# Splitting the forms of a pair of weight blocks as three tiles of 1024 columns and one of 512

## The chip, the core and the metric

The kernel runs on one core of a Trainium2 chip, in one launch. The metric is the device time of one execution in microseconds, here the median of several runs. TensorE (PE in the profile, its weight loads PEld) does the matmuls, VectorE is DVE, ScalarE is ACT, GpSimd is POOL, and SyncE (SP) issues most DMAs.

## The reference

The kernel computes one layer of a hybrid encoder on 512 positions of width 1024, in float32:

```python
x1 = x  + RMSNorm( W_out( sig(a_ret) * W_ret_o(Retention(h)) + sig(a_sgu) * W_sgu_o(SGU(h)) ) ),  h = RMSNorm(x)
y  = x1 + RMSNorm( ConvGatedMLP( RMSNorm(x1) ) )
```

`h @ w_in` gives the queries, keys, values and gate of the retention branch, the two inputs `u` and `sv` of the SGU branch, and the two merge gates. The SGU branch is `(gelu(u) * mixed(sv)) @ w_sgu_o`, the gated MLP is `gelu(a) * b` of an up projection (2 x 2816 columns, with a convolution of width 3), followed by `w_down`. Nearly all of the time is matrix products of 512 positions with weights.

## The kernel before

**High and low parts.** A float32 product is made of three matmuls of float32r operands. `split(hi, lo, src)` (line 119 and the copy of line 100) rounds a tile on ScalarE, `hi = copy(src)`, and takes the rest on VectorE, `lo = src - hi`. Each weight tile in use is a pair (hi, lo), and each product does hi by hi, hi by lo and lo by hi.

**Weights in a ring.** The weights come as 146 blocks of 128 x 1024 float32, each by one DMA of 512 KB into one of four `raw` tiles, issued on SyncE. Their halves go into a ring of nine slots of 1088 columns (tag `w4`). `w_get` hands out the units of a list in the order of their use, and starts on the units ahead as far as the ring has room: nine slots in general. A whole block takes two slots (one for hi, one for lo).

**Pairs.** Where two weight blocks that stand side by side make two tiles of outputs, the class `Pair` uses a scheme with 7 products in place of 8, in the manner of Strassen and Winograd. Its weights are seven forms of 128 x 512: B11, B21, the sums T1 = B11 + B12, T3 = B12 + B22, T2 = T1 + B22, T4 = T2 + B21, and B22. Each form is used in one product of 12 matmuls of 128 x 256 (line 926), in the order B11, B21, T1, T2 (`part1`), T3 (`part2`), T4, B22 (`part3`). There are 20 pairs, 1680 matmuls in all:

- The middle stage, some 200 to 343 us, has four pairs for `u` (U1, U2, U3 in the table `MIDDLE` are their parts 1, 2 and 3) and four for the gate (G1, G2, G3), interleaved with whole blocks (W) and small steps (M, Y). U11 and U12 are part 1 of the second and third pair for `u`.
- The gate stage, some 343 to 403 us, has four `gated_pair`: part 1, a whole block (`f_block`, lines 300 to 302), part 2, half a block, part 3, the other half.
- The up projection, some 490 to 648 us, has eight pairs in the same manner (`COUPLES`, each a pair and two whole blocks).

Then comes the down projection (line 1372), whose weights `w_down` splits (dh, dl); the change doesn't touch its code.

**How a form is made before.** `w_form` takes one ring slot for each of the seven forms, with lo and hi side by side in it, and splits 512 columns at a time. B11 brings the two DMAs of the pair. T1 and T3 are added on VectorE when T1 is due; T2 then too, on VectorE in the pairs for `u` and in the couples, on GpSimd in the gate pairs of both stages. T4 is added when it is due, on the same engine, in the place of T2.

**What sets the order.** The program is written in the order of use, and a scheduler of the compiler sets the order of each engine's instructions by its own estimate of when they may start. On one engine they then go in that order, and an instruction that has to wait for another engine (a copy on ScalarE, a slot that TensorE still reads) holds up those behind it. Part 1's products accumulate in PSUM banks; the fourth product (T2, called S2 after its second operand) is added to the bank of the first, so it must wait for ScalarE's copy of the first out of PSUM.

Of the kernel before, what the change touches and what calls it, by code (L numbers as in the profile page):

```python
# [13 lines left out]
ALU = mybir.AluOpType  # L14

P = 128
D = 1024
S = 512
# [34 lines left out]
def tile_block(ctx: ExitStack, tc, xT, x, wall, par, cs, wsp, bsp, gpost, gffn, out):  # L53
# [71 lines left out]
    FORMS = ("B11", "B21", "T1", "T2", "T3", "T4", "B22")  # L125
    units = []
    i = 0
    while i < NW:
# [6 lines left out]
        elif i == U0:  # L135
            us, gs = ([[(f, k + n * m) for f in FORMS] for n in range(KD // 2)] for k, m in ((U0, 2), (GATE0, 4)))
            ws = [("blk", GATE0 + 4 * (n // 2) + 2 + n % 2) for n in range(KD)]
            for what, n in MIDDLE:
                units += {"W": lambda: ws[n : n + 1], "U1": lambda: us[n][:4], "U2": lambda: us[n][4:],
                          "G1": lambda: gs[n][:4], "G2": lambda: gs[n][4:]}.get(what, list)()  # L140
            i = GATE0 + 2 * KD
        elif GATE0 <= i < GATE1:
            units += pair[:4] + [("blk", i + 2)] + pair[4:] + [("blk", i + 3)]
            i += 4
        elif i == UP0 + 2 * COUPLES[0][0]:
            for a, b in COUPLES:
                pair = [(f, UP0 + 2 * a) for f in FORMS]
                units += pair[:4] + [("blk", UP0 + 2 * b)] + pair[4:] + [("blk", UP0 + 2 * b + 1)]
# [45 lines left out]
    def w_form(form, i):  # L194

        if form == "B11":
            a, b = raw_tile(), raw_tile()
            nc.sync.dma_start(a, wall[i])
            nc.sync.dma_start(b, wall[i + 1])
            w_raw["B11"], w_raw["B12"] = a[:, :S], a[:, S:]  # L200
            w_raw["B22"], w_raw["B21"] = b[:, :S], b[:, S:]
        elif form == "T1":
            t = raw_tile()
            w_raw["T1"], w_raw["T2"], w_raw["T3"], w_raw["T4"] = t[:, :S], t[:, S:], w_raw["B12"], t[:, S:]
            nc.vector.tensor_add(w_raw["T1"], w_raw["B11"], w_raw["B12"])
            nc.vector.tensor_add(w_raw["T3"], w_raw["B12"], w_raw["B22"])
            eng = nc.vector if i < GATE0 or i >= UP0 else nc.gpsimd
            eng.tensor_tensor(out=w_raw["T2"], in0=w_raw["T1"], in1=w_raw["B22"], op=ALU.add)
        elif form == "T4":
            eng = nc.vector if i < GATE0 or i >= UP0 else nc.gpsimd  # L210
            eng.tensor_tensor(out=w_raw["T4"], in0=w_raw["T2"], in1=w_raw["B21"], op=ALU.add)
        w = slot("wf", 0, 1088)
        lo, hi = w[:, AT_64 : AT_64 + S], w[:, S + AT_192 : 2 * S + AT_192]
        split(hi, lo, w_raw[form])
# [66 lines left out]
    def w_size(u):  # L281
        return 2 if u[0] in ("blk", "q", "t") or u[0][0] == "s" else 1
# [626 lines left out]
    class Pair:  # L909
# [9 lines left out]
        def product(self, b, act, first, w=None):  # L919
            wh, wl = w or w_get()  # L920
# [21 lines left out]
        def part1(self):  # L942
# [3 lines left out]
            def second():  # L946
# [732 lines left out]
```

## Time and profile before

| what | value |
|---|---|
| median of 3 runs | 783.18 us (782.7 to 783.85) |
| the profiled execution, span | 782.6 us, 13472 instructions |
| TensorE clock granted, mean | 0.997 of full speed |
| TensorE busy | 774.5 us, 99% of the span |
| VectorE, ScalarE, GpSimd busy | 639.5, 485.2, 103.5 us |

In the profile a group of instructions is named by its line, engine and operation, with output and inputs by their names in the program: `wf` is a form's slot, `wh` and `wl` the halves of a whole block, `raw` a weight tile as it came, `u`, `sig` and `c` a pair's output tiles, `ps` a PSUM bank. A row such as `x140 | 107.0, 774` means 140 of them, busy for 107.0 us together, 774 ns the mean of one; what follows is idle time ahead of them and who ended it. In a timeline, a row has the start, the length in us, the engine, the line and the operation; "x2" is two that follow one another directly. Lengths of neighbours overlap, so the step from one start to the next is what an operation takes up.

### The profile page before, as it was taken

What the parts mean: (1) busy time and instruction counts of PE and PEld (TensorE: products, weight loads), DVE (VectorE), ACT (ScalarE), POOL (GpSimd) and SP (SyncE); (2) the same over time, 40 slices, a digit from 0 to 9 for tenths busy, and PEclk for the clock granted to TensorE, in tenths of its full rate; (3) what the DMA queues carried; (4) which work ended last, traced back from release to release, by engine and by line L of the source; (5) the groups of instructions that cost most, each with busy time, mean ns of one, the idle gap of its engine ahead of it and who ended that gap; (6) DMA issues with size and microseconds to landing.
All of it is one profiled execution on the core that took longest, in us unless ns stands there. A gap on an engine that the chain in (4) does not pass through costs nothing.

```text
span 782.6 us, 13472 instructions
## 1 busy us (share of the span) xinstructions
PE 774.5 (99%) x5139; PEld 720.7 (92%) x5139; DVE 639.5 (82%) x1093; ACT 485.2 (62%) x878; POOL 103.5 (13%) x132
## 2 busy tenths in 40 slices
PE   9999999999999999999999999999999999999996
PEld 8888998998999999999998998999999998999996
DVE  6567987789789988877765679989999889886987
ACT  7555568688466766644454686657777568644542
POOL 0040001130021102033211200001111012200001
PEclk9999999999999999999999999999999999999998
DMA  8783224453223233233459120435555375733344
GB/s 288 271 246 102 81 82 162 108 122 108 81 91 126 82 122 121 83 110 106 138 171 337 54 81 28 124 107 141 142 148 149 108 199 111 171 114 107 109 162 162
DMA packets 35889, 104.80 MB, mean 134 GB/s; under 512 B 4400, under 2 KB 6320, under 8 KB 35824
## 3 DMA queue, kind: packets, MB, share of 16 engines
q1 hardware_dynamic: 27936, 87.81, 34.0%
q0 software_dynamic: 7024, 14.95, 9.0%
q10 hardware_dynamic: 864, 1.18, 0.4%
q8 instruction: 40, 0.66, 0.4%
q14 instruction: 25, 0.20, 0.1%
HBM read 91.34 MB, written 4.19 MB: 122 GB/s over the span
## 4 chain that ended last, share of the span: by engine, by line
PE 92%; DVE 3%; DMA 3%; issue 1%; ACT 0%; POOLq 0%; DVEq 0%; POOL 0%; ACTq 0%
PE ps L926 24%; PE ps L300 12%; PE ps L302 12%; PE ps L301 12%; PE ps L1372 7%; PE ps L755 5%; PE ps L634 4%; PE ps L636 4%; PE ps L635 4%; DMA raw<-wall 3%; PE ps L1109 2%; PE ps L1108 2%; PE ps L1107 2%; DVE dl L119 1%; PE ps L997 1%
## 5 line engine op out<-in xcount | busy, mean ns | idle before, releaser
L119 DVE TENSOR_TENSOR wl<-raw,wh 128x1024 fp32r<-128x1024 f32 (+1 forms) x84 | 96.0, 1152 | 54.3 <-issue 19.1
L100 ACT ACTIVATE wf<-raw 128x512 fp32r<-128x512 f32 x140 | 85.6, 625 | 67.3 <-PE ps L301 19.4
L926 PE MATMUL ps<-sh,wf 128*128 128x256 f32 x640 | 117.4, 276 | 0.1
L119 DVE TENSOR_TENSOR wf<-raw,wf 128x512 fp32r<-128x512 f32 x140 | 107.0, 774 | 9.2 <-ACT wf L100 8.6
L926 PEld LDWEIGHTS ps<-sh,wf 128*128 128x128 f32 x640 | 101.9, 192 | 1.1 <-ACT sig L100 0.5
L100 ACT ACTIVATE wh<-raw 128x1024 fp32r<-128x1024 f32 (+2 forms) x88 | 84.8, 977 | 28.5 <-DMA raw<-wall 14.0
L300 PE MATMUL ps<-h2h,wh 128*128 128x512 f32 (+1 forms) x256 | 90.6, 354 | 0.0
L301 PE MATMUL ps<-h2l,wh 128*128 128x512 f32 (+1 forms) x256 | 90.4, 353 | 0.0
L302 PE MATMUL ps<-h2h,wl 128*128 128x512 f32 (+1 forms) x256 | 90.4, 353 | 0.0
L926 PE MATMUL ps<-sl,wf 128*128 128x256 f32 x320 | 88.0, 275 | 0.0
L926 PEld LDWEIGHTS ps<-sl,wf 128*128 128x128 f32 x320 | 61.4, 192 | 0.4
L1372 PE MATMUL ps<-dh,fh 128*128 128x256 f32 x216 | 59.6, 276 | 0.3 <-DVE yy L1409 0.3
L1372 PE MATMUL ps<-dl,fh 128*128 128x256 f32 x216 | 59.5, 275 | 0.0
L1372 PE MATMUL ps<-dh,fl 128*128 128x256 f32 x216 | 59.4, 275 | 0.0
L100 ACT ACTIVATE dh<-raw 128x768 fp32r<-128x768 f32 (+1 forms) x36 | 33.6, 950 | 33.8 <-DVE raw L231 15.2
L302 PEld LDWEIGHTS ps<-h2h,wl 128*128 128x128 f32 x256 | 48.6, 190 | 5.1
L301 PEld LDWEIGHTS ps<-h2l,wh 128*128 128x128 f32 x256 | 48.6, 190 | 4.5
L300 PEld LDWEIGHTS ps<-h2h,wh 128*128 128x128 f32 x256 | 48.6, 190 | 4.5
L926 PE MATMUL ps<-xh,wf 128*128 128x256 f32 x288 | 52.2, 275 | 0.0
L636 PE MATMUL ps<-wh,xl 128*128 128x512 f32 x128 | 48.5, 379 | 0.0
L635 PE MATMUL ps<-wl,xh 128*128 128x512 f32 x128 | 48.5, 379 | 0.0
L634 PE MATMUL ps<-wh,xh 128*128 128x512 f32 x128 | 48.5, 380 | 0.0
(343 smaller groups left out, 2171.6 us busy)
## 6 DMA issues: line engine op xcount, KB each, us to landing
raw<-wall SPq DMA_DIRECT2D x144, 512.0 KB, 3.7
x<-x SPq DMA_DIRECT2D x24, 256.0 KB, 6.0
fl<-gp POOLq DMA_DIRECT2D x12, 256.0 KB, 3.8
swap<-qkraw POOLq DMA_DIRECT2D x16, 128.0 KB, 4.8
x<-x POOLq DMA_DIRECT2D x8, 256.0 KB, 2.3
fl<-fs POOLq DMA_DIRECT2D x8, 256.0 KB, 4.3
xT<-xT SPq DMA_DIRECT2D x7, 256.0 KB, 5.0
xT<-xT POOLq DMA_DIRECT2D x4, 256.0 KB, 4.1
```

Of the source, the lines that this page charges most:

```text
L100: return nc.scalar.activation(out=o, in_=i, func=AF.Copy)
L119: low[0] = nc.vector.tensor_sub(lo, src, as32(hi)).ins
L300: nc.tensor.matmul(o, ah, bh, start=start, stop=False, skip_group_check=skip)
L301: nc.tensor.matmul(o, ah, bl, start=False, stop=False, skip_group_check=skip)
L302: pe_last[0] = nc.tensor.matmul(o, al, bh, start=False, stop=stop, skip_group_check=skip).ins
L634: nc.tensor.matmul(acc[t], xh[k][:, c], turns(wh[:, f]), start=k == 0, stop=False)
L635: nc.tensor.matmul(acc[t], xh[k][:, c], turns(wl[:, f]), start=False, stop=False)
L636: part_end[0] = nc.tensor.matmul(acc[t], xl[k][:, c], turns(wh[:, f]), start=False, stop=k == KD - 1)
L755: nc.tensor.matmul(bank[t], a_[:, c], turns(w_[:, f]), start=first and k == i == 0, stop=last and k == 3 and i == 2, skip_group_check=True,)
L926: self.last = nc.tensor.matmul(o, w_[:, c], a_, start=first and k == n == 0, stop=k == 3 and n == 2, skip_group_check=True,)
L1107: nc.tensor.matmul(o, ah, turns(bh), start=k == 0, stop=False)
L1372: nc.tensor.matmul(o, a_[:, c], turns(w_[:, f]), start=j == t == i == 0, stop=j == DP - 1 and i == 2 and n not in (M2, M3, M4), skip_group ...
```

## The change

The seven forms become four units: `B1` (B11 and B21 side by side, 1024 columns), `T12` (T1 and T2), `T34` (T3 and T4) and `B22`. The host puts B21 behind B11 and B12 behind B22, so that B1 is the first DMA's tile as it came. A unit of 1024 columns takes two slots, hi and lo, like a whole block, and is split by one copy and one subtraction. B22 stays as it was. A pair still takes seven slots in all, with the same DMAs and the same adds on the same engines. T3 and T4 are now written into the raw tile of B1, once that has been split, and T2 is no longer overwritten.

A whole unit is now split at once. So the first product needs B21's half split with B11's, T1's product needs T2 added, and T3's needs T4 added; a unit's two slots come free when its second product has read them. T4's half is used in part 3 only, so T34's two slots are held from part 2 to part 3, across the parts of the other pair that stand between them in the middle stage.

```diff
-    FORMS = ("B11", "B21", "T1", "T2", "T3", "T4", "B22")
+    FORMS = ("B1", "T12", "T34", "B22")
...
-                          "G1": lambda: gs[n][:4], "G2": lambda: gs[n][4:]}.get(what, list)()
+                          "G1": lambda: gs[n][:2], "G2": lambda: gs[n][2:]}.get(what, list)()
...
-        if form == "B11":
-            a, b = raw_tile(), raw_tile()
+        eng = nc.vector if i < GATE0 or i >= UP0 else nc.gpsimd
+        if form == "B1":
+            a, b = w_raw["a"], w_raw["b"] = raw_tile(), raw_tile()
             nc.sync.dma_start(a, wall[i])
             nc.sync.dma_start(b, wall[i + 1])
-            w_raw["B11"], w_raw["B12"] = a[:, :S], a[:, S:]
-            w_raw["B22"], w_raw["B21"] = b[:, :S], b[:, S:]
-        elif form == "T1":
-            t = raw_tile()
-            w_raw["T1"], w_raw["T2"], w_raw["T3"], w_raw["T4"] = t[:, :S], t[:, S:], w_raw["B12"], t[:, S:]
-            nc.vector.tensor_add(w_raw["T1"], w_raw["B11"], w_raw["B12"])
-            nc.vector.tensor_add(w_raw["T3"], w_raw["B12"], w_raw["B22"])
-            eng = nc.vector if i < GATE0 or i >= UP0 else nc.gpsimd
-            eng.tensor_tensor(out=w_raw["T2"], in0=w_raw["T1"], in1=w_raw["B22"], op=ALU.add)
-        elif form == "T4":
-            eng = nc.vector if i < GATE0 or i >= UP0 else nc.gpsimd
-            eng.tensor_tensor(out=w_raw["T4"], in0=w_raw["T2"], in1=w_raw["B21"], op=ALU.add)
-        w = slot("wf", 0, 1088)
-        lo, hi = w[:, AT_64 : AT_64 + S], w[:, S + AT_192 : 2 * S + AT_192]
-        split(hi, lo, w_raw[form])
+            w_raw["B22"], w_raw["B12"] = b[:, :S], b[:, S:]
+            raw = a
+        elif form == "T12":
+            raw = w_raw["t"] = raw_tile()
+            nc.vector.tensor_add(raw[:, :S], w_raw["a"][:, :S], w_raw["B12"])
+            eng.tensor_tensor(out=raw[:, S:], in0=raw[:, :S], in1=w_raw["B22"], op=ALU.add)
+        elif form == "T34":
+            raw = w_raw["a"]
+            nc.vector.tensor_add(raw[:, :S], w_raw["B12"], w_raw["B22"])
+            eng.tensor_tensor(out=raw[:, S:], in0=w_raw["t"][:, S:], in1=raw[:, S:], op=ALU.add)
+        if form == "B22":
+            w = slot("wf", 0, 1088)
+            lo, hi = w[:, AT_64 : AT_64 + S], w[:, S + AT_192 : 2 * S + AT_192]
+            raw = w_raw["B22"]
+        else:
+            hi, lo = slot("wf", AT_192), slot("wf", AT_64)
+        split(hi, lo, raw)
         return hi, lo
...
-        return 2 if u[0] in ("blk", "q", "t") or u[0][0] == "s" else 1
+        return 1 if u[0] == "B22" else 2
...
+        def halves(self):
+            hi, lo = w_get()
+            return [(hi[:, f], lo[:, f]) for f in (slice(0, S), slice(S, 2 * S))]
...
-            o = self.product(0, self.x(0, T0), True)
+            w = self.halves()
+            o = self.product(0, self.x(0, T0), True, w[0])
             copy(two(c0[:, T0]), o)
-            second()
-            self.product(2, self.s("S1"), True)
-            o = self.product(0, self.s("S2"), False)
+            second(w[1])
+            w = self.halves()
+            self.product(2, self.s("S1"), True, w[0])
+            o = self.product(0, self.s("S2"), False, w[1])
...
-            o = self.product(0, self.s("S3"), False)
+            w = self.halves()
+            o = self.product(0, self.s("S3"), False, w[0])
...
-            self.w = w_get(), w_get()
+            self.w = w[1], w_get()
```

Line numbers move a little: the product's matmul is line 933 after the change, the adds into a pair's outputs of lines 948, 957, 963, 972, 976 and 978 are 955, 966, 973, 982, 986 and 988.

The scheduler's order moves with it. The first place is VectorE in the middle stage, around 250 to 257 us, where the weights of U12 are made while the pairs before it end. The names' numbers differ between the two programs. Before, `wf_2755` and `wf_2763` are B11 and B21 of U12, `wf_2783` and `wf_2799` its T1 and T2:

```order
L963 TENSOR_TENSOR u_2566<-ps_2569,u_2566 128x256
L119 TENSOR_TENSOR wf_2748<-raw_2587,wf_2748 128x512
L119 TENSOR_TENSOR wf_2755<-raw_2751,wf_2755 128x512
L205 TENSOR_TENSOR raw_2779<-raw_2751 128x512
L948 TENSOR_TENSOR sig_2758<-ps_2761,sig_2758 128x256
L119 TENSOR_TENSOR wf_2763<-raw_2752,wf_2763 128x512
L206 TENSOR_TENSOR raw_2751<-raw_2751,raw_2752 128x512
L208 TENSOR_TENSOR raw_2779<-raw_2779,raw_2752 128x512
L119 TENSOR_TENSOR wf_2783<-raw_2779,wf_2783 128x512
L957 TENSOR_TENSOR sig_2758<-sig_2758,rbc_567 128x256
L119 TENSOR_TENSOR wf_2799<-raw_2779,wf_2799 128x512
```

After, `wf_2737` is the low half of B1 and `wf_2770` that of T12:

```order
L973 TENSOR_TENSOR u_2548<-ps_2551,u_2548 128x256
L1023 TENSOR_TENSOR u_2296<-mix_2701,u_2296 128x512
L205 TENSOR_TENSOR raw_2766<-raw_2732,raw_2733 128x512
L119 TENSOR_TENSOR yl_2800<-u_2295,yh_2799 128x512
L955 TENSOR_TENSOR sig_2727<-ps_2730,sig_2727 128x256
L206 TENSOR_TENSOR raw_2766<-raw_2766,raw_2733 128x512
L119 TENSOR_TENSOR wf_2710<-raw_2582,wf_2710 128x512
L966 TENSOR_TENSOR sig_2727<-sig_2727,rbc_567 128x256
L119 TENSOR_TENSOR yl_2804<-u_2296,yh_2803 128x512
L119 TENSOR_TENSOR wf_2737<-raw_2732,wf_2736 128x1024
L1001 SCALAR_TENSOR_TENSOR add_2997<-rws_1911,part,bst_2208 128x128
L119 TENSOR_TENSOR wf_2770<-raw_2766,wf_2769 128x1024
```

B11's split was the third operation from the u row on and B21's the sixth; now both are one operation, the tenth, behind T1, T2 and two splits for the next stage (`yl`).

The second place is ScalarE at the end of the middle stage, around 325 to 329 us. The last row of the first listing, and the second of the other, copies the first product of a gated pair out of PSUM (`sig<-ps`); the sigmoids belong to the pair before it. Before:

```order
L100 ACTIVATE wf_3670<-raw_3457 128x512
L1061 ACT_TABLE_LOAD
L1061 ACTIVATE sig_3435<-sig_3435 128x512
L100 ACTIVATE yh_3661<-u_3249 128x512
L1061 ACTIVATE sig_3436<-sig_3436 128x512
L100 ACTIVATE sig_3665<-ps_3667 128x256
```

After:

```order
L100 ACTIVATE wf_3616<-raw_3422 128x512
L100 ACTIVATE sig_3611<-ps_3613 128x256
L1071 ACT_TABLE_LOAD
L1071 ACTIVATE sig_3387<-sig_3387 128x512
L1071 ACTIVATE sig_3388<-sig_3388 128x512
L100 ACTIVATE yh_3607<-u_3207 128x512
```

The copy now stands ahead of the table load and the two sigmoids.

The third place is TensorE itself, just there: its matmuls are in the same order throughout, except that in this one place the product S2, which waits for that copy, has moved. Before, the three matmuls of the first step of a whole block come ahead of it:

```order
L926 MATMUL ps_3669<-sh_1687,wf_3495 128x256
L300 MATMUL ps_3748<-yh_2828,wh_3581 128x512
L301 MATMUL ps_3748<-yl_2829,wh_3581 128x512
L302 MATMUL ps_3748<-yh_2828,wl_3582 128x512
L926 MATMUL ps_3667<-sh_603,wf_3539 128x256
```

After, S2 (`ps_3613`) follows directly on the product before it:

```order
L933 MATMUL ps_3615<-sh_1687,wf_3485 128x256
L933 MATMUL ps_3615<-sl_1688,wf_3485 128x256
L933 MATMUL ps_3615<-sh_1687,wf_3486 128x256
L933 MATMUL ps_3613<-sh_603,wf_3485 128x256
L933 MATMUL ps_3613<-sl_604,wf_3485 128x256
```

S2 moved forward by three matmuls, and the block's first step behind its twelve. SyncE's and GpSimd's orders are the same before and after.

21 lines of the change are left out of this document (9 added, 12 removed).

## The prediction, as it was recorded before the changed kernel had run

> **What bounds the kernel now.** I read the page's busy times first, then TensorE's own waits, then the windows of 20 us, and last the rows at the few places where TensorE loses time.
>
> ```profile
> PE 774.5 (99%) x5139; PEld 720.7 (92%) x5139; DVE 639.5 (82%) x1093; ACT 485.2 (62%) x878; POOL 103.5 (13%) x132
> PE 92%; DVE 3%; DMA 3%; issue 1%; ACT 0%; POOLq 0%; DVEq 0%; POOL 0%; ACTq 0%
> ```
>
> TensorE is busy for 774.5 of 782.6 us and has 92% of the chain of waits. A busy TensorE may still be slow, so I look at its pace. The chain of waits has the Pair products, line 926, in long runs without a break:
>
> ```profile
> 210.36 5.36 PE ps L926 x48
> ```
>
> 5.36 / 48 is 111.7 ns from one matmul to the next, and the rows further down step by 0.11 or 0.12 as well: the matmuls go at their own pace and no weight comes late. The change leaves 5139 matmuls of the same shapes, so it can only win what TensorE loses beyond that pace. The waits of TensorE's weight loads that touch line 926 are two:
>
> ```profile
> PEld ps L926 <- ACT sig L100: 0.5, 1, 0.5
> PEld ps L926 <- ACT u L100: 0.2, 1, 0.2
> ```
>
> The windows (PE busy, PEld busy, DVE busy, ACT busy and POOL busy, then the granted clock, the DMA share and GB/s) show where a late weight would hurt first:
>
> ```profile
> 240.00:260.00 20.00, 20.00 (x161) 19.41 (x160) 19.75 (x33) 15.36 (x26) 2.48 (x2) 1.00 0.19 63
> 340.00:360.00 20.00, 20.00 (x137) 18.71 (x136) 15.59 (x22) 9.43 (x16) 5.89 (x4) 1.00 0.31 106
> 480.00:500.00 20.00, 20.00 (x117) 18.19 (x116) 20.00 (x32) 12.65 (x22) 0.00 (x0) 1.00 0.29 95
> ```
>
> VectorE is full in 240 to 260 and in 480 to 500 us, yet TensorE loses nothing there: the weights are split some us ahead of their use, and VectorE's load is work done early. So the change matters by when the halves are ready, not by how busy VectorE is.
>
> **The change part by part.** Matmuls, DMA issues, bytes and adds stay as they are. Three times in each of the 20 pairs, two splits of 512 columns become one of 1024: 60 operations fewer on VectorE and 60 fewer on ScalarE.
>
> ```profile
> L119 DVE TENSOR_TENSOR wf<-raw,wf 128x512 fp32r<-128x512 f32 x140 | 107.0, 774 | 9.2 <-ACT wf L100 8.6
> L119 DVE TENSOR_TENSOR wl<-raw,wh 128x1024 fp32r<-128x1024 f32 x72 | 88.5, 1229 | 52.6 <-issue 19.1 <-ACT wh L100 14.6 <-PE ps L926 6.3
> ```
>
> By these means a merge saves 2 x 774 - 1229 = 319 ns on VectorE: 60 of them are 19 us of busy time. The means count overlapped ends twice. By starts of neighbours, two splits take 1.20 (250.50 to 251.70 in the next rows) and one of 1024 takes 1.13 (257.85 to 258.98): 0.07 saved, 4 us in all. I take nearer 4, as the starts hold no overlap. On the time this counts 0, and ScalarE's part too, at 62% busy: TensorE's matmuls lie over both, and if they did not, VectorE's would be worth at most 19 us.
>
> The price of the change is when a half comes. B11's product used to need a split of 512 columns; now it needs one of 1024, into two ring slots instead of one, and T3 and T4 hold two slots until part 3 has used T4. By the slots' addresses and the matmuls' times, every form in the gate stage and the couples finds its slot free over 8 us ahead of need. The exceptions are U11 and U12, whose B1 is split while another pair still holds its slots. U12 comes when VectorE is full. VectorE's rows of before there (start, length, line):
>
> ```profile
> 250.16 0.41 DVE L963 TENSOR_TENSOR u<-ps,u 128x256 f32<-128x256 f32 x1
> 250.50 1.28 DVE L119 TENSOR_TENSOR wf<-raw,wf 128x512 fp32r<-128x512 f32 x2
> 251.70 0.68 DVE L205 TENSOR_TENSOR raw<-raw 128x512 f32<-128x512 f32 x1
> 252.30 0.42 DVE L948 TENSOR_TENSOR sig<-ps,sig 128x256 f32<-128x256 f32 x1
> 252.63 0.68 DVE L119 TENSOR_TENSOR wf<-raw,wf 128x512 fp32r<-128x512 f32 x1
> ...
> 257.85 1.22 DVE L119 TENSOR_TENSOR wl<-raw,wh 128x1024 fp32r<-128x1024 f32 x1
> 258.98 0.68 DVE L978 TENSOR_TENSOR u<-u,rbc 128x512 f32<-128x512 f32 x1
> ```
>
> TensorE's rows: the last read of the slot that B1's low half goes into, the first read of that half (the third matmul of U12), the first read of T12's low half, and the loss at 261.
>
> ```profile
> 252.94 0.28 PE L926 MATMUL ps<-sl,wf 128*128 128x256 f32 x1
> ...
> 257.40 0.39 PE L926 MATMUL ps<-xh,wf 128*128 128x256 f32 x2
> ...
> 260.08 0.39 PE L926 MATMUL ps<-sh,wf 128*128 128x256 f32 x2
> ...
> 261.09 0.63 PE L926 MATMUL ps<-sh,wf 128*128 128x256 f32 x2
> 261.55 0.28 PE L926 MATMUL ps<-sl,wf 128*128 128x256 f32 x1
> ```
>
> Before, B11's low half is the second split of the row at 250.50, ready at 251.78, 5.6 us ahead of 257.40. After, the program order puts eight operations between the u row of 250.16 and B1's split. An operation of 512 costs 0.60 from start to start (251.70 to 252.30), one of 256 0.33. So: 250.16 + 0.33 + 3 x 0.60 = 252.30, where the sig operation (now line 955) also starts in before; then 0.33 + 0.60 + 0.60 + 0.33 + 0.60 gives 254.76; the split ends 1.22 later, at 255.98. The slot is free after 252.94. B1 is 1.4 us early. T12's split follows after a short add (0.26) at 256.15 and ends at 257.4, 2.7 us ahead of 260.08. ScalarE's copies come earlier: it has only 15.36 of 20 us in this window. At U11 the slot's last read and the half's first read are these:
>
> ```profile
> 227.21 0.28 PE L926 MATMUL ps<-sl,wf 128*128 128x256 f32 x1
> ...
> 231.68 0.39 PE L926 MATMUL ps<-xh,wf 128*128 128x256 f32 x2
> ```
>
> The slot is free 4.4 us ahead; the same walk there puts the split's end near 229.1, an estimate, and leaves 2.6 us. **So the cost here is 0, between 0 and what a slip beyond 1.4 us would bring.**
>
> The 0.24 lost at 261 is a wait for ScalarE's copy of u out of PSUM, itself behind a gelu:
>
> ```profile
> 259.70 0.63 ACT L1052 ACTIVATE u<-u 128x512 f32<-128x512 f32 x1
> ...
> 260.92 0.37 ACT L100 ACTIVATE u<-ps 128x256 f32<-128x256 f32 x1
> ```
>
> The gelu waits for VectorE's u at 258.98. In the new order that u has three operations between it and T12's split (257.3 + 0.33 + 0.33 + 0.60 = 258.6), and the copy stands ahead of the weight copy, so it may end at 260.2 and the loss goes; if VectorE slips by 1 us, it stays. Between -0.24 and +0.3; I take -0.1.
>
> The larger loss is at 328, where TensorE waits for a copy that ScalarE makes behind a table load and two sigmoids:
>
> ```profile
> 325.11 1.28 ACT L1061 ACT_TABLE_LOAD   x1
> 326.40 0.64 ACT L1061 ACTIVATE sig<-sig 128x512 f32<-128x512 f32 x1
> ...
> 327.67 0.64 ACT L1061 ACTIVATE sig<-sig 128x512 f32<-128x512 f32 x1
> 328.21 0.36 ACT L100 ACTIVATE sig<-ps 128x256 f32<-128x256 f32 x1
> ```
> ```profile
> 327.94 0.38 PE L301 MATMUL ps<-yl,wh 128*128 128x512 f32 x1
> 328.15 0.38 PE L302 MATMUL ps<-yh,wl 128*128 128x512 f32 x1
> 328.62 0.38 PE L926 MATMUL ps<-sh,wf 128*128 128x256 f32 x1
> ```
>
> From 328.15 to 328.62 is 0.47 where such a matmul takes 0.21 (327.94 to 328.15), and the first of line 926 runs 0.38 for 0.28: 0.35 lost. In the new order the copy is ahead of the table load and could end near 325.5; TensorE wants it at 327.72, as the S2 product now goes before the three matmuls of the whole block. Term: -0.35, at worst 0.
>
> At the entry of the down projection both engines' orders shift, with little slack:
>
> ```profile
> 683.77 1.22 DVE L119 TENSOR_TENSOR dl<-raw,dh 128x1024 fp32r<-128x1024 f32 x1
> ```
> ```profile
> 684.84 0.28 PE L1372 MATMUL ps<-dh,fh 128*128 128x256 f32 x1
> 685.05 0.38 PE L1372 MATMUL ps<-dl,fh 128*128 128x256 f32 x1
> ```
>
> The split ends at 684.99 and TensorE reads it at 685.05, 0.2 late for its pace by that matmul and the next. One operation of 512 more or less ahead of it is 0.6; so -0.2 to +0.5, and I take 0.
>
> T2 and T4 stay on GpSimd in the gate pairs, and now a whole T12 or T34 waits for them:
>
> ```profile
> L208 POOL TENSOR_TENSOR raw<-raw,raw 128x512 f32<-128x512 f32 x8 | 13.3, 1660 | 90.6 <-DMA raw<-wall 74.2 <-DVE raw L205 16.4
> ```
>
> T1's split waits 1.66 us longer than before; against over 8 us of slack, and 20.00 of TensorE beside 15.59 of VectorE in 340 to 360, that costs 0. In the first couple, with VectorE full, the nearest use is that of the whole block between the forms:
>
> ```profile
> 498.41 1.22 DVE L119 TENSOR_TENSOR wl<-raw,wh 128x1024 fp32r<-128x1024 f32 x1
> ```
> ```profile
> 502.43 0.38 PE L302 MATMUL ps<-h2h,wl 128*128 128x512 f32 x1
> ```
>
> It is ready at 499.63, 2.8 us early, and the operations ahead of it keep their sum less the merges: 0.
>
> Sum: -0.1 - 0.35 + 0 + 0 = -0.45 on the profiled 782.6, or 782.15. The median of before stands 0.58 above its profiled execution (783.18), so I say **782.7 us**.
>
> **The rivals.**
>
> *First: the coarser split comes late (slower).* It decides from the point where B1's low split of U12 starts later than 256.18 (257.40 less 1.22), 1.4 us after my walk. For it: VectorE is 19.75 of 20 busy there, its operations go in program order, and yl and sig operations ahead of the split each wait for another engine. Five operations of 0.60 more ahead of it are 3.0 us, 1.6 lost at U12 and, by the same count, as much at U11; with the loss at 328 still gone this is 782.6 + 3.2 - 0.35, or 786.0 at the median. Against it: at both places the walk leaves room. The Trainium skill's Perfetto Trace Analysis, section Optimizing Scalar/DVE Operations, speaks for this rival: where ScalarE or VectorE are not saturated but cause bubbles on other engines, breaking instructions up may let work finish sooner, and this change does the reverse. By the trace, the bubbles at 261 and 328 come from copies behind other operations, not from long splits, so I leave the chance small.
>
> *Second: all removable losses go.* 0.35, 0.24, 0.2, and some 0.66 at 726, where TensorE waits for VectorE's yy:
>
> ```profile
> 726.47 0.38 PE L1372 MATMUL ps<-dh,fh 128*128 128x256 f32 x1 [0.27 <-DVE yy L1409]
> ```
>
> The row before starts at 725.93, so 0.54 pass for 0.11 of work, and smaller delays lie ahead. Together 1.45 us: 781.7. Against it: nothing of the change lies within 60 us of 726.
>
> *Third: VectorE's time counts after all.* If TensorE's pace in the two full windows were set by VectorE, the merges there (about nine) would be worth 9 x 0.32 = 2.9 us: 780.3. Against it: TensorE shows 20.00 in both.
>
> *Fourth: GpSimd's adds become the last event in the gate pairs.* T12 would have to be over 8 us later than now, and two adds of 1.66 are 3.3. Were the slack shorter than these by 1 us in each of the 8 pairs, 8 us would be lost: 791.
>
> **How the numbers follow.** The forecast has 0.66, the first rival 0.13, the second 0.15, the third 0.03, the fourth 0.03. Runs of before go from 782.7 to 783.85, so I call 0.2% (1.57 us, below 781.61 or above 784.75) the least that can be told from no change. The second rival lies next to that bound; I give a third of it, 0.05, to faster. So faster is 0.05 + 0.03 = 0.08, slower 0.13 + 0.03 = 0.16, the same 0.76. The forecast's own range goes from 782.0 to 783.7 (its terms -1.0 to +0.5, and the scatter of runs). The range given takes in the second rival with scatter below and half of the first above: 781.5 to 785.0.
>
> **What would show it right or wrong.** Right: TensorE's wait for the sig copy near 328 is gone; VectorE's busy time falls by 4 to 19 us and TensorE's stays at 774; no wait of line 933 on a split (wf from line 119 or 100) of over 0.2 us. The copy of u near 261 shows which end of that term holds. Wrong: TensorE waits for VectorE's split at 231.7 or 257.4, new gaps from 660 to 690, or matmuls of the Pair at another step than 111.7 ns, which nothing here can foretell since their operands only lie in other slots.

## The result, and the profile after

The change made the kernel slower, by 6 us where no measurable change was forecast.

| | before | after |
|---|---|---|
| median | 783.34 us (4 runs, 782.7 to 783.85) | 789.51 us (4 runs, 788.38 to 791.06) |
| ratio | | 1.0078 (95% interval 1.0066 to 1.0091) |
| span of the profiled execution | 782.6 us | 787.5 us |
| start of the last matmul in it | 775.37 us | 780.32 us |

Two executions of the experiments below, with granted clocks of 0.79 and 0.85, took 1499 and 893 us and are left out of all medians.

The page after has these busy times:

```profile
PE 775.7 (99%) x5139; PEld 721.2 (92%) x5139; DVE 633.6 (80%) x1033; ACT 476.9 (61%) x818; POOL 105.6 (13%) x132
```

VectorE and ScalarE did get 60 operations and 5.9 and 8.3 us of work less, and TensorE's own work is the same within 1.2 us. The step between matmuls is 0.11 us in the rows below, as before. What came are waits, in the view of TensorE's waits (what it waited for, us in total, how often, the longest):

```profile
PE ps L933 <- ACT u L100: 1.6, 2, 1.2
PE ps L405 <- PEq L1676: 0.8, 1, 0.8
PE ps L933 <- ACT sig L100: 0.7, 1, 0.7
PE ps L423 <- ACT xh L340: 0.4, 1, 0.4
PE ps L1382 <- DVE e L1418: 0.4, 1, 0.4
PE ps L1398 <- DVE wl L119: 0.3, 1, 0.3
...
```

The windows of the middle stage after, to be read beside the row of 240 to 260 us in the prediction:

```profile
220.00:240.00 20.00, 19.60 (x172) 19.33 (x171) 14.15 (x21) 12.58 (x20) 0.33 (x1) 1.00 0.32 107
240.00:260.00 20.00, 19.33 (x149) 18.38 (x149) 18.94 (x28) 11.17 (x16) 2.87 (x2) 1.00 0.24 80
260.00:280.00 20.00, 18.77 (x146) 17.94 (x145) 16.87 (x28) 14.56 (x21) 3.42 (x2) 1.00 0.41 130
```

TensorE is idle in all three, and VectorE and ScalarE are *less* busy in 240 to 260 than before (18.94 for 19.75, 11.17 for 15.36). The stage is not short of either engine: both wait for something.

Counting from the starts of the matmuls what each step took beyond its usual length gives where the 5 us of the profiled execution are:

| where (us after) | waits for | lost before | lost after |
|---|---|---|---|
| 235 | ScalarE's copy of u out of PSUM | 0 | 0.67 |
| 252 and 257 | ScalarE's copy of sig | 0 | 1.13 |
| 263 | ScalarE's copy of u | 0.24 | 1.50 |
| 328 | ScalarE's copy of sig | 0.35 | 0 |
| couples: 497, 586, 606 | ScalarE's copies of c | 0 | 0.90 |
| down projection: 685 to 704 | VectorE's splits wl, dl | 0.21 | 1.03 |
| down projection: 725 to 731 | VectorE's e and yy | 0.63 | 1.27 |

So 3.06 us came in the middle stage, 0.35 went at its end, and 2.36 came in the couples and the down projection.

The wait at 263 can be followed back. TensorE's row, and ScalarE's rows ahead of the copy that it waits for:

```profile
262.77 0.27 PE L933 MATMUL ps<-sh,wf 128*128 128x256 f32 x1
264.28 0.38 PE L933 MATMUL ps<-sh,wf 128*128 128x256 f32 x1 [1.23 <-ACT u L100]
```
```profile
260.17 1.06 ACT L100 ACTIVATE wh<-raw 128x1024 fp32r<-128x1024 f32 x1 [2.80 <-DMA raw<-wall]
261.24 1.28 ACT L1062 ACT_TABLE_LOAD   x1
262.54 0.63 ACT L1062 ACTIVATE u<-u 128x512 f32<-128x512 f32 x1
263.07 0.36 ACT L100 ACTIVATE sig<-ps 128x256 f32<-128x256 f32 x1
263.34 0.62 ACT L1062 ACTIVATE u<-u 128x512 f32<-128x512 f32 x1
263.86 0.37 ACT L100 ACTIVATE u<-ps 128x256 f32<-128x256 f32 x1
```

No weight of the pair is late. ScalarE stood for 2.80 us on the copy of the next *whole block* (W4 in the stage's order), whose DMA had not landed; the table load, two gelus and the copy out of PSUM are behind it in ScalarE's order. That DMA was issued right behind a split on VectorE, first SyncE's row, then VectorE's (the u row is that of 250.16 before, shown in the prediction):

```profile
256.58 0.33 SPq L176 DMA_DIRECT2D raw<-wall  x1
```
```profile
252.79 0.42 DVE L973 TENSOR_TENSOR u<-ps,u 128x256 f32<-128x256 f32 x1
...
255.86 0.69 DVE L119 TENSOR_TENSOR wf<-raw,wf 128x512 fp32r<-128x512 f32 x1
```

The split at 255.86 is that of G11's B22, the last to read the raw tile that the block's DMA writes. Before, the same tile's last split was the first of the two at 250.50, and these are SyncE's and ScalarE's rows of before:

```profile
251.24 0.33 SPq L176 DMA_DIRECT2D raw<-wall  x1
```
```profile
255.96 1.05 ACT L100 ACTIVATE wh<-raw 128x1024 fp32r<-128x1024 f32 x1
257.03 1.28 ACT L1052 ACT_TABLE_LOAD   x1
```

The DMA left 5.3 us earlier, and ScalarE did not wait for it. Of these 5.3 us, 2.63 had come already by the u row (252.79 for 250.16). The other 2.73 are VectorE's new order: B22's split started 0.34 us after the u row before, and 3.07 after, as five operations now stand between, the adds of U12's T1 and T2 among them. B22 itself is a form of 512 columns in both kernels. TensorE ran 1.7 us later after than before at this place, so the slip proper is some 3.6 us.

The wait at 235 has the same chain one block earlier. W3's DMA left at 228.50 (225.53 before), at the end of the split of G10's B22. VectorE had stood for 2.35 us ahead of that, on the T1 add of U11 at 225.33, which waited for its own DMA. ScalarE then stood for 3.17 us, until 232.02, on W3's copy; the gelu ahead of the late copy of u waited for VectorE too, which had come to that u only after W3's split.

### The profile page after: what moved, and what is told of

It is laid out like the page before. It is cut to its first block, busy times and chain, and to the rows that moved or that the text cites. A ratio compares the mean times of both kernels' runs of the same rounds, so it can differ in the third digit from the quotient of the medians.

```text
span 787.5 us, 13361 instructions
## 1 busy us (share of the span) xinstructions
PE 775.7 (99%) x5139; PEld 721.2 (92%) x5139; DVE 633.6 (80%) x1033; ACT 476.9 (61%) x818; POOL 105.6 (13%) x132
## 5 line engine op out<-in xcount | busy, mean ns | idle before, releaser
L119 DVE TENSOR_TENSOR wf<-raw,wf 128x1024 fp32r<-128x1024 f32 x80 | 95.2, 1192 | 11.6 <-ACT wf L100 9.9
L100 ACT ACTIVATE wf<-raw 128x1024 fp32r<-128x1024 f32 x80 | 75.1, 946 | 46.0 <-DVE raw L206 13.6
```

The lines of the kernel that those rows point to most:

```text
L100: return nc.scalar.activation(out=o, in_=i, func=AF.Copy)
L119: low[0] = nc.vector.tensor_sub(lo, src, as32(hi)).ins
```

## The experiments

Each kernel was run beside the kernel before on the same chip; the ratios are to that, and a cost in us is the ratio times the time of before unless medians are named. All of them compute the whole reference. In the middle stage, "W4's DMA" is the one of the whole block above.

### By stage

The seven forms were put back, with the layout of before, in all stages but one.

```diff
+    def first(i):
+        return [(f, i) for f in (("B1", "T12") if stage(i) in MERGED else ("B11", "B21", "T1", "T2"))]
+
+    def rest(i):
+        return [(f, i) for f in (("T34", "B22") if stage(i) in MERGED else ("T3", "T4", "B22"))]
```

The middle stage alone:

> Only the eight pairs of the middle stage have the four units of the change; the gate stage and the couples have the seven forms of before, with the layout of before. Theory A (late raw tiles: B22's split comes later, so the raw tile it holds, the next whole block's DMA and ScalarE's copy of that block come later, and the copies out of PSUM that stand behind it in ScalarE's order make TensorE wait at 235, 252 and 263 us): the three waits stay, TensorE loses about 3.2 us there, and the time is 3 to 4 us above before, 786 to 787.5. Rival B (splits of 1024 columns are too coarse wherever they stand): the cost goes by the number of pairs, 8 of 20, so about 2.4 us, and the couples carry as much. Rival C (the down projection's new order carries it): no more than 1.5 us above before.

The gate stage alone:

> Only the four pairs of the gate stage have the four units. Theory A: no wait there, as every raw tile and slot is free over 8 us ahead; the same time as before within 1 us. Rival B: 4 of 20 pairs, about 1.2 us slower. Rival C: the down projection's order is as in before, so the same as before.

The couples alone, and one more execution of them, with its profile:

> Only the eight pairs of the up projection have the four units. Theory A: small waits for copies out of PSUM at the first and two later couples (0.4, 0.25, 0.25 us), and in the down projection what its new order brings (about 1.4 us against before): 1.5 to 2.5 us slower, 785 to 786. Rival B: about 2.4 us slower, with the waits inside the couples. Rival C: 4 us or more slower, with the waits from 690 us on.

> The couples alone have the four units, once more, for a profile. The two or three waits for copies of c near 497, 586 and 606 us (some 0.3 each) and a down projection that loses some 1 us more than before, if those are what makes the couples' share of about 2 us.

| units of 1024 in | median | ratio | 95% interval |
|---|---|---|---|
| middle stage | 785.99 | 1.0031 | 1.0019 to 1.0043 |
| gate stage | 783.93 | 1.0004 | 0.9995 to 1.0014 |
| couples | 786.18 (783.9 to 786.6) | 1.0027 | 1.0015 to 1.0040 |

The middle stage alone brings back the waits at 235, 252 and 263 us (0.74, 1.40 and 1.54 us) and costs 2.4 us; the gate stage costs nothing that can be told. That speaks against rival B, a price per pair: it asked for 1.2 us from the gate stage's four pairs, and the interval there ends at 1.1. The couples cost 2.1 us, and their runs lie apart, near 784 to 785 and near 786.5. The profiled execution, 784.49 us, has waits of 0.38, 0.28 and 0.25 us at 494, 583 and 603 and no new wait in the down projection; what it expected there did not come. So the rest of the couples' cost is not in every execution. No long execution of this kernel has a profile; one of a kernel with the same couples, further down, has the loss in the down projection.

### B22 first

The split that released the raw tile was moved ahead.

```diff
-    FORMS = ("B1", "T12", "T34", "B22")
+    FORMS = ("B1", "T12", "B22", "T34")
...
-            w = self.halves()
+            b22, w = w_get(), self.halves()
```

> The change as it is, but B22 is made ahead of T34 (units B1, T12, B22, T34; the products keep their order), so that its raw tile comes free earlier and the next block's DMA can start earlier. Theory A: the DMAs of the whole blocks in the middle stage are issued some 3 to 5 us earlier, ScalarE no longer waits for them, and most of the 3.2 us at 235 to 263 us comes back: 785.5 to 787.5. Rival B: nothing changes, 789 to 790, as the splits are as coarse. Rival C: nothing changes by 680 us; what happens later depends on the order there.

788.94 us, ratio 1.0076 (1.0059 to 1.0093): nothing gained, against theory A's number. But W4's DMA was not issued 3 to 5 us earlier either, only 1.4: with the order changed, it takes the raw tile of T34, and that split is now the late one. ScalarE waited 4.86 us for the DMA (it landed at 260.1) and TensorE 2.78 us more than its step for the copy behind. The DMA left at the end of that split. The expectation's step failed, and the chain showed again, with another split at its head.

### Which unit

T3 and T4 apart again, one slot each, in every pair; T3 and T4 alone together; and all seven apart, but in the layout of the change:

```diff
-        elif form == "T34":
-            raw = w_raw["a"]
-            nc.vector.tensor_add(raw[:, :S], w_raw["B12"], w_raw["B22"])
-            eng.tensor_tensor(out=raw[:, S:], in0=w_raw["t"][:, S:], in1=raw[:, S:], op=ALU.add)
+        if form in ("T34", "T3"):
+            nc.vector.tensor_add(w_raw["a"][:, :S], w_raw["B12"], w_raw["B22"])
+        if form in ("T34", "T4"):
+            a = w_raw["a"]
+            eng.tensor_tensor(out=a[:, S:], in0=w_raw["t"][:, S:], in1=a[:, S:], op=ALU.add)
```

> B1 and T12 stay units of 1024 columns, but T3 and T4 are split apart again, one slot each, in all 20 pairs; layout and raw tiles as in the change. Theory A, made sharper (the ring is one slot short: T34 keeps T3's half until T4 is used in part 3, so the other pair's last unit, B22 or with B22 first T34, must wait for B1's release, its raw tile comes free late, and the whole block's DMA and everything behind it on ScalarE are late): the waits at 235, 252 and 263 us go, and the time is 783.5 to 785.5. Rival B (splits of 1024 are too coarse): two of three merges are left, so two thirds of the 6 us, 787 to 788.5.

> Only T3 and T4 are split together; B11, B21, T1 and T2 have a slot each again, in all 20 pairs, with the layout and raw tiles of the change. Theory A: the slot that T34 keeps is enough, the waits near 235 to 263 us stay for the most part, and the time is 786 to 789. Rival B: a third of the 6 us, 785 to 786. A third theory D (B1 and T12 held for two products each are what makes the ring short): no waits in the middle stage, 783 to 784.5.

> Seven forms of 512 columns, one slot each, as before, but with the change's layout of the raw tiles (B21 beside B11, T3 and T4 written into B1's tile). It tells whether the layout and the raw tiles' lifetimes carry the cost. Theory A and rival B: the same as before within 1 us, 783 to 784.5. Rival E (T4 in B1's raw tile instead of T12's makes the raw tiles come free later): 786 or more, with ScalarE waiting for the whole blocks' DMAs.

| units of 1024 | median | ratio | 95% interval |
|---|---|---|---|
| B1, T12 | 783.31 | 0.9999 | 0.9990 to 1.0009 |
| T34 | 786.35 | 1.0034 | 1.0022 to 1.0046 |
| none (layout alone) | 783.53 | 1.0008 | 0.9999 to 1.0018 |
| all three (the change) | 789.51 | 1.0078 | 1.0066 to 1.0091 |

Taking T34 apart gives back the whole 6 us, though 40 of the 60 merges stay. This is its view of TensorE's waits in full; none of the middle stage's is there:

```profile
PE ps L415 <- PEq L1689: 0.8, 1, 0.8
PE ps L949 <- ACT c L101: 0.2, 1, 0.2
PE ps L1395 <- DVE yy L1432: 0.2, 1, 0.2
```

W4's DMA and ScalarE's copy there:

```profile
249.68 0.33 SPq L183 DMA_DIRECT2D raw<-wall  x1
```
```profile
254.25 1.08 ACT L101 ACTIVATE wh<-raw 128x1024 fp32r<-128x1024 f32 x1
```

Rival B (coarse splits) is out, and rival E (the layout) is out for the waits of the middle stage: the layout alone loses nothing from 230 to 270 us. It is not out for the couples' share. Three of the layout's ten executions took 785.3 to 785.6 us, as the couples' long ones did, while none of the 71 executions of before that ran beside the experiments took more than 784.6. So some 2 us can come in part of the executions with no split merged at all; the layout's profiled execution is a short one, and where its long ones lose the time is not shown. T34 alone costs 2.7 us, but not where the change does: it has a wait of 0.92 us at 235, none at 252 or 263 (W4's DMA leaves at 251.96), and loses 2.2 us in the down projection, where before lost 0.8.

### Is it the ring?

The kernel before with eight slots, the change with ten, and a control; the tenth slot's room comes from two of the six temporaries.

```diff
-        return sb.tile([P, 1088], F32R, tag="w4", bufs=9, name=nm(n))[:, at : at + w]
+        return sb.tile([P, 1088], F32R, tag="w4", bufs=8, name=nm(n))[:, at : at + w]
```
```diff
-        return sb.tile(list(shape), F32, tag="tmp", bufs=6, name=nm(n))
+        return sb.tile(list(shape), F32, tag="tmp", bufs=4, name=nm(n))
```

> The kernel before, with seven forms of 512 columns, but a ring of eight slots instead of nine; the look-ahead is as before, so that the unit that used to take the ninth slot has to wait for a release. Theory A (the change makes the ring one slot short): waits for ScalarE's copies appear near 235 to 263 us although no split has been merged, with the middle stage's second whole block issued at 254 us or later instead of 251.2; 785.5 to 789. Rival B (coarse splits): none of this, 783 to 784.5, as every split still has 512 columns.

> The change with a ring of ten slots; the room for the tenth is taken from the ring of temporaries (four tiles of 512 columns instead of six). Theory A: the waits at 235, 252 and 263 us go; if four temporaries are enough, 783 to 785.5. Rival B: 788 to 790. The next kernel tells what the temporaries cost.

> The change with nine slots and only four temporaries, as a control of the kernel with ten slots. Theory A: the waits at 235 to 263 us stay, 788 us or more, and the difference to the kernel with ten slots is the price of the missing slot, 3 us or more. Rival B: the same time as with ten slots within 1 us.

Eight slots in the kernel before: 792.08 us, 1.0112 (1.0083 to 1.0140). It is dearer than the change, but the waits are elsewhere (167, 322 to 330, 402, the couples, 692), none from 230 to 270: a missing slot as such does not make the change's pattern. Ten slots: 809.94 us, 1.0333 (1.0318 to 1.0348), where every theory had said less than 791. The control with nine slots and four temporaries has 792.61 us, 1.0112 (1.0095 to 1.0129), and all the waits of the change at 235 to 264 (3.6 us together). With ten slots the order on each engine is another throughout, and copies out of PSUM in the gate stage and the couples stand behind operations that wait for GpSimd and VectorE (1.4 us in most pairs). These two kernels tell that a larger ring is no cure; what a tenth slot alone is worth they don't tell.

### B1 or T12 beside T34

In the middle stage alone, and then T34 apart there alone:

```diff
-M = (("B1", "T12"), ("T34", "B22"))
+X = (("B1", "T1", "T2"), ("T34", "B22"))
+Y = (("B11", "B21", "T12"), ("T34", "B22"))
```

> In the middle stage alone, B1 and T34 are units of 1024 columns, T1 and T2 have a slot each; gate stage and couples have seven forms, all in the layout of the change. Theory A (T34 makes B22 wait for the release of the slots that B11 and B21 hold, and B1 gives them back one product, 1.34 us, later than B11 would): the waits at 252 and 263 us are there, with the second whole block's DMA at 254 us or later, and the time is 785.5 to 787. Theory F (T12 is what matters beside T34): the DMA comes by 252.5, no wait of over 0.5 us at 252 or 263, 783 to 785.

> The same with T12 and T34 as units and B11 and B21 apart. Theory A: B11's slot comes free one product earlier, the DMA is issued by 252.5 us, and the waits at 252 and 263 us are under 0.5 us together; 783.5 to 785. Theory F: the waits are there, 785.5 to 787.

> The change, with T3 and T4 apart in the middle stage alone; gate stage and couples keep all four units. If the cost adds up by stage, the middle stage's 2.4 us go and the couples' share stays: 785 to 787.5. If the cost behind the middle stage only follows from its delays: 783 to 784.5.

| kernel | median | ratio | 95% interval |
|---|---|---|---|
| B1 and T34, middle | 783.49 | 1.0001 | 0.9992 to 1.0011 |
| T12 and T34, middle | 785.51 | 1.0031 | 1.0017 to 1.0044 |
| the change, T34 apart in the middle | 784.78 (783.7 to 786.0) | 1.0020 | 1.0010 to 1.0030 |

Theory A's last form fell: B1 with T34 costs nothing, and T12 with T34 costs 2.4 us, but at 235 and 278 us (0.91 and 1.19), not at 252 and 263. Neither couple makes the pattern of all three. The third kernel's median lies between its two ranges. None of the middle stage's three waits is left, and the couples' share stays in part of the executions: the profiled one, a long one, loses 0.9 us in the couples and 2.6 from 687 to 728, and the nine runs lie near 783.8 and near 786, like the couples alone.

### The raw tiles

What sets most of the kernels so far apart is the time of W4's DMA:

| kernel | W4's DMA issued at | TensorE lost, 250 to 265 us |
|---|---|---|
| B1, T12 (T3, T4 apart) | 249.68 | 0 |
| layout alone | 249.99 | 0 |
| before | 251.24 | 0.24 |
| T34 alone | 251.96 | 0 |
| T12 and T34, middle | 252.52 | 0 |
| B1 and T34, middle | 252.87 | 0 |
| before, eight slots | 253.34 | 0 |
| B22 first | 255.18 | 4.0 |
| the change, middle only | 256.44 | 2.9 |
| the change | 256.58 | 2.6 |
| the change, four temporaries | 256.82 | 2.9 |
| the change, ten slots | 257.61 | 0 |

The last row is against the pattern. With ten slots TensorE ran later here (U12's first product starts at 261.45, and at 258.87 in the change). ScalarE came to W4's copy only at 262.87 and did not wait for the DMA. So what counts is the DMA's time against ScalarE's, and not the time alone. An order like this may also hide a common cause, so the DMA was made early without touching a split: a raw tile of its own for the middle stage's whole blocks, then a fifth raw tile for all, both with four temporaries, which the control above has too.

```diff
-        raw = raw01[i] if i < 2 else raw_tile()
+        raw = raw01[i] if i < 2 else raw_own() if GATE0 <= i < GATE0 + 16 else raw_tile()
```
```diff
-        return sb.tile([P, 1024], F32, tag="raw", bufs=4, name=nm("raw"))
+        return sb.tile([P, 1024], F32, tag="raw", bufs=5, name=nm("raw"))
```

> The change with four temporaries, as in the control (792.6 us), and a raw tile of its own for the eight whole blocks of the middle stage, so that their DMAs wait for no split of a pair's forms. Theory G (the late DMA of the whole block is the cause: ScalarE waits for it, and the copies out of PSUM stand behind): the block's DMA is issued before 250 us, ScalarE does not wait for it, TensorE's waits at 235, 252 and 263 us fall from 3.5 to under 1.5 us, and the time is 2 us or more below the control: 788.5 to 790.6. Theory H (the late splits themselves hold the copies up, the DMA only goes along): the waits stay within 0.7 us, 792 to 793.5.

> The change with four temporaries and five raw tiles for all weights. Theory G: as with the blocks' own tile in the middle stage, 788.5 to 790.6, or less if raw tiles are short in the couples and the down projection too. Theory H: 792 to 793.5.

| kernel | median | lost at 235 | at 252 and 257 | at 263 |
|---|---|---|---|---|
| control | 792.61 | 0.69 | 1.35 | 1.54 |
| own tile for the blocks | 791.02 | 0 | 1.29 | 0.62 |
| five raw tiles | 790.49 | 0 | 0 | 0 |

With the blocks' own tile W4's DMA left at 233.69, and the wait at 235 and 0.9 of that at 263 went; the wait at 252 stayed and one of 0.4 us came at 279, so the sum of the three is 1.9 and not under 1.5, and the time just misses its range (1.6 us below the control, not 2). By the operations' names, ScalarE's order from 200 to 300 us is that of the control in this kernel, and VectorE's is too up to 261; so no new order took the wait at 235 away, but the earlier DMA, that of W3 (206.45 for 228.50 in the change). With five tiles, and all three units as in the change, the middle stage loses nothing. Its windows, W4's DMA, the split of G11's B22 and ScalarE's rows:

```profile
240.00:260.00 20.00, 20.00 (x164) 19.49 (x163) 19.80 (x32) 14.81 (x22) 1.21 (x1) 1.00 0.26 90
260.00:280.00 20.00, 20.00 (x159) 19.36 (x158) 19.39 (x28) 13.41 (x20) 2.57 (x2) 1.00 0.28 96
```
```profile
247.20 0.33 SPq L176 DMA_DIRECT2D raw<-wall  x1
```
```profile
251.92 0.68 DVE L119 TENSOR_TENSOR wf<-raw,wf 128x512 fp32r<-128x512 f32 x1
```
```profile
253.97 1.06 ACT L100 ACTIVATE wh<-raw 128x1024 fp32r<-128x1024 f32 x1
255.04 1.28 ACT L1062 ACT_TABLE_LOAD   x1
256.44 0.64 ACT L1062 ACTIVATE u<-u 128x512 f32<-128x512 f32 x1
256.98 0.37 ACT L100 ACTIVATE sig<-ps 128x256 f32<-128x256 f32 x1
258.50 0.63 ACT L1062 ACTIVATE u<-u 128x512 f32<-128x512 f32 x1 [1.16 <-DVE u L988]
259.04 0.37 ACT L100 ACTIVATE u<-ps 128x256 f32<-128x256 f32 x1
```

The copy out of PSUM ends at 259.4 where the change had 264.2. B22's split still stands behind the adds for T12, but the DMA left 4.7 us ahead of it. ScalarE's order is again that of the control; VectorE's differs in several places. So theory G holds for the middle stage: the raw tiles are what the change is short of there. The blocks' tile accounts for 235 and most of 263; the wait at 252 goes with the pairs' own tiles: G11's second DMA leaves at 231.91 with five tiles, at 235.23 with the blocks' own tile and at 235.90 in the change. The whole kernel gains only 2.1 us on the control (790.49, ratio 1.0092, 1.0074 to 1.0110), though 3.6 us went in the middle stage: it has new waits of 2.5 us from 406 to 418 us and keeps the couples' 0.7 each that came with four temporaries. So its time within theory G's range is in part luck.

## Why the prediction was wrong, step by step

**What bounds the kernel: right.** TensorE's work and its step stayed, and the 5.9 us that VectorE saved (near the 4 us taken, far from 19) and ScalarE's 8.3 bought nothing.

**"Matmuls, DMA issues, bytes and adds stay as they are": the step that failed.** Their number stays; their time does not. The sum had a term for when a ring slot comes free and when a half is ready, and none for when a raw tile comes free. W4's block goes into the raw tile of G11's B22. That split came 5.4 us later, 2.63 by VectorE's earlier delays and 2.73 by its new order, and the DMA with it. The new order stood in the listing of VectorE, which the prediction walked for B1's split and not for B22's. Five tiles take all of the middle stage's waits away with B1, T12 and T34 still merged; that is shown. That T34 has to be one of the units for the waits at 235, 252 and 263 is shown too (none without it, and 783.31). Why it has to be is not shown: the tile that was late is not T34's own.

**"ScalarE's copies come earlier: it has only 15.36 of 20 us in this window": wrong in kind.** A share of busy time was taken for readiness. ScalarE had time, but its next operation waited 2.80 us for a DMA, with the copies out of PSUM behind it. The copies were priced one by one from VectorE's walk; the whole block's copy, two places ahead of the gelu, had no term.

**B1's split at U12 and U11: cost 0, right.** B1's low half ended at 258.62 and was first read at 259.09, so it was 0.5 us early, not 1.4; T12's was early as well. The walk's own steps held: from the u row to B1's split it had 4.60 us, and 4.61 were measured. What slid was its start, the u row, which it took over from before. TensorE waited for no split of a pair in the middle stage.

**The loss at 261, "between -0.24 and +0.3": mis-sized.** It went from 0.24 to 1.50, and two new ones of its kind, 0.67 at 235 and 1.13 at 252 to 257, were in no term.

**The loss at 328, -0.35: right.** The copy came ahead of the table load and the wait is gone.

**The entry of the down projection, -0.2 to +0.5: half right.** The 0.2 at 685 went, but 1.03 came at 691 and 704 and 0.64 more at 725 to 731, outside the range. The first couple, priced at 0, lost 0.38 at 497.

**GpSimd's adds: right for the gate stage.** It costs 0.04% (interval -0.05 to 0.14%), as its slack promised. The middle stage's gate pairs had no such term: ScalarE stood there for 3.55 us, until 242.91, on GpSimd's T2, though TensorE did not wait before 252.

**The signs of being right: they came true all the same.** The wait at 328 was gone, VectorE's busy time fell by 5.9 us, and no product of a pair waited for a split. None of them looked at a whole block's DMA, so they could not show this failure; of the signs of being wrong, only a new gap came, at 691 where 660 to 690 was named.

**The rivals.** The first had the sign and less than half the size (2.8 of 6.2 us), but not the mechanism. Its condition was met, as B1's split started at 257.40, after 256.18; but TensorE's need came 1.7 us later too, and it did not wait. The rule of the Trainium skill's Perfetto Trace Analysis, section Optimizing Scalar/DVE Operations, which stood beside it, that breaking instructions up may let work finish sooner where ScalarE or VectorE aren't saturated but hold up other engines, had the right direction by luck. VectorE had 19.75 of 20 us in that window before, and B1 and T12 stayed coarse at no cost (ratio 0.9999), so coarseness as such was not the price. The second, third and fourth rivals did not occur.

**From the profiled execution to the median.** The prediction added 0.58 us to 782.6. The runs beside the experiments list their spans: before has a median span of 781.6 us for 783.4 us of time (21 runs), so 1.8 us lie outside the span, and the profiled execution was about 1 us longer than the median one. The change has 2.16 us outside the span. This is why the medians differ by 6.2 us and the two profiled spans by only 4.9.

**What stays open.** Why all three units are needed for the waits at 252 and 263, while B1 with T34 costs nothing and T12 with T34 costs as much in other places: each of these kernels has its own order on ScalarE and VectorE. The wait at 235 was taken away with both orders kept; for those at 252 and 263 no run separated VectorE's order from the tiles. The couples' and the down projection's share, some 2 us, was not taken apart, and the layout alone has as much in three of ten executions. Five raw tiles were run only with four temporaries, which cost 0.7 us in each couple but the first. No version beat the kernel before: the best, with B1 and T12 as units, is the same.

## What to carry to other kernels

When an edit makes units of staged data larger, list every buffer on the way, the raw tiles as well as the ring, and ask for each which operation now releases it and which DMA waits for that; a count of DMAs that stays the same says nothing on when they go. Then follow that DMA's consumer on its engine and see what stands behind it: here a copy for a later block held up the copies out of PSUM, on an engine that was 56% busy. Check the order of the engine that frees the buffer for that buffer's last reader, and not only for the operations that changed. The one merge that had to go was T34, whose halves are used furthest apart (T3 in part 2, T4 in part 3). That the longer holding of its buffers is the reason is a guess that no run here shows: beside B1 alone, in the middle stage, it cost nothing (ratio 1.0001).

## What the runs showed of the hardware

In the kernel with B22 first, 2.89 us passed on TensorE from one matmul's start to the next, 2.62 of them idle, and then it ran at a granted clock of 0.50. These are windows of its profile (span, PE busy, PEld, DVE, ACT, POOL busy, granted clock, DMA share, GB/s):

```profile
260.00:261.36 1.36, 1.36 (x14) 1.36 (x13) 0.32 (x2) 1.21 (x2) 0.00 (x0) 1.00 0.00 0
264.25:265.25 1.00, 0.99 (x4) 1.00 (x5) 0.97 (x3) 1.00 (x2) 0.00 (x0) 0.50 0.96 336
265.25:266.25 1.00, 1.00 (x7) 1.00 (x6) 0.47 (x1) 0.42 (x1) 0.00 (x0) 0.50 0.87 201
266.25:267.25 1.00, 1.00 (x7) 1.00 (x6) 0.00 (x0) 0.03 (x1) 0.00 (x0) 0.51 0.63 254
267.25:268.25 1.00, 1.00 (x11) 1.00 (x11) 0.00 (x0) 1.00 (x2) 0.00 (x0) 1.00 0.23 94
```

The clock is 0.50 from 264.25 to some 267.2, and eleven matmuls there have a step of 213 or 214 ns instead of 112: 1.1 us on top of the stop itself. After the change's stop of 1.51 us at 262.77 only one matmul was slow. But the length of a stop does not settle it. The kernel before with eight slots has a longer one, 2.97 us from 692.12, and its clock stayed at 1.00:

```profile
695.10 0.38 PE L1372 MATMUL ps<-dl,fh 128*128 128x256 f32 x1 [2.70 <-DVE dl L119]
```
```profile
695.10:696.10 1.00, 1.00 (x9) 1.00 (x10) 1.00 (x4) 0.00 (x0) 0.00 (x0) 1.00 0.07 20
696.10:697.10 1.00, 1.00 (x12) 1.00 (x11) 1.00 (x2) 0.00 (x0) 0.00 (x0) 1.00 0.97 336
```

What made the difference between the two stops is not shown.

A split of 1024 columns on VectorE took longer while GpSimd added. In the change, G11's two splits took 1.97 and 2.23 us where one alone takes 1.22:

```profile
241.99 1.97 DVE L119 TENSOR_TENSOR wf<-raw,wf 128x1024 fp32r<-128x1024 f32 x1
243.88 0.41 DVE L986 TENSOR_TENSOR sig<-ps,sig 128x256 f32<-128x256 f32 x1
244.22 2.23 DVE L119 TENSOR_TENSOR wf<-raw,wf 128x1024 fp32r<-128x1024 f32 x1
```
```profile
241.27 1.60 POOL L206 TENSOR_TENSOR raw<-raw,raw 128x512 f32<-128x512 f32 x1 [20.94 <-DVE raw L205]
244.09 1.27 POOL L210 TENSOR_TENSOR raw<-raw,raw 128x512 f32<-128x512 f32 x1 [1.22 <-DVE wf L119]
```

GpSimd was adding T2 from 241.27 to 242.87 and T4 from 244.09 to 245.36, in the time of the two splits. GpSimd's operations had 0.88 and 1.14 us left when the splits started, and the splits took 0.75 and 1.01 us more than one alone: 0.13 us less than that in both cases.
